# A matrix product with rotary embedding: weight chunks and the first four input tiles loaded in turn, and the early casts shared out anew

## The chip, the cores and the metric

The kernel runs on one core of one Trainium2 chip. The metric is the device time of one execution in microseconds (us). The span of a profile is some 2 us shorter than the device time of the same execution.

## The reference

```python
# x 16 x 512 x 768, weight 768 x 768, cos and sin 512 x 64, n_heads 12, all float32
y = np.matmul(x, weight).reshape(batch, seq, n_heads, head_dim)
y1, y2 = halves of the last axis of y
out1 = y1 * cos1 - y2 * sin1
out2 = y2 * cos2 + y1 * sin2
return np.concatenate([out1, out2], axis=-1).reshape(batch, seq, hidden)
```

## The kernel before

The input is cut into 64 tiles of 128 rows, taken as 32 pairs; (n, s) is tile s of pair n. A tile is loaded, cast to fp16, transposed by TensorE into PSUM in six blocks, copied back to SBUF, mostly by ScalarE, and multiplied with six weight chunks, each 128 x 768 (20 of the later tiles are transposed by VectorE instead). One tile with one chunk is a "tile-chunk": a 512-column and a 256-column product. VectorE then multiplies with cos and sin (the "rope"), GpSimd adds, and a store follows. The program order is fixed by hand. The change is in the start, where tiles one to four (pairs 0 and 1) meet weights that are still arriving. In this text tile five is (2, 0), tile six is (2, 1), and the weight chunks have the numbers 0 to 5.

```python
for n in (0, 1):
    load_pair(n)                     # tiles one to four
load_w(0, 0, 0, 256)                 # chunk 0 in two pieces
load_w(0, 0, 256, H)
for t, e in CHUNKS[1:]:
    load_w(t, e)                     # chunks 1 to 5
... cos, sin, then tiles five and on, all on one queue
warm(10)                             # products with zeros
cast(0, 0, nc.vector)
cast(0, 1, nc.scalar)
transpose(0, 0, nc.vector)           # the engine is that of the copy back
warm(2)
transpose(0, 1, nc.scalar)
cast(1, 0, nc.vector)
cast(1, 1, nc.scalar)
warm(2)
transpose(1, 0, nc.vector)
warm(3)
for c0, c1 in ((0, 256), (256, H)):
    cast_w(0, 0, c0, c1)
    mm(0, 0, 0, 0, c0, c1)
    mm(0, 1, 0, 0, c0, c1)
    if c0 == 0:
        transpose(1, 1, nc.scalar)
for k, c in enumerate(CHUNKS[1:]):
    cast_w(*c)
    if k < 2:
        mm(1, 0, *CHUNKS[k])
    mm(0, 0, *c)
    mm(0, 1, *c)
    if 1 < k < 4:
        mm(1, 0, *CHUNKS[k])
... VectorE prepares cos and sin
rope_pair(0)
upto("cast", 6)                      # ScalarE casts tiles five and six
for c in CHUNKS[4:]:
    mm(1, 0, *c)
for c in CHUNKS[:3]:
    mm(1, 1, *c)
upto("turn", 5)                      # tile five: transposes, ScalarE's copy back
for c in CHUNKS[3:]:
    mm(1, 1, *c)
rope_pair(1)
for n in range(2, NP):               # from here on as in the kernel after
    ...                              # tile five's product, tile six's transposes, ...
```

## Time and profile before

| what | before |
|---|---|
| time, median of three runs | 155.65 us (155.53 to 155.98) |
| span of the profile | 153.0 us |
| TensorE / VectorE / GpSimd / ScalarE busy | 96% / 85% / 81% / 50% |
| first VectorE cast of a whole weight chunk began | 9.66 us |
| last weight cast began | 13.64 us |
| tile five's cast on ScalarE began | 15.34 us |
| tile five's product on TensorE began | 17.97 us |

A line of the timeline has the start, the length, the engine (PE is TensorE's products, PEld its weight loads, DVE VectorE, ACT ScalarE), the source line, the operation with output and input, how many were merged, and in brackets the idle time before it with what ended it. A line of the chain of waits has the start, the length and who held the chain. The ends of products are modelled, starts are recorded; so where a small gap of TensorE matters below, it is taken from starts.

### The profile page before, as it was taken

What the parts mean: (1) busy time and instruction counts of PE and PEld (TensorE: products, weight loads), DVE (VectorE), ACT (ScalarE), POOL (GpSimd) and SP (SyncE); (2) the same over time, 40 slices, a digit from 0 to 9 for tenths busy, and PEclk for the clock granted to TensorE, in tenths of its full rate; (3) what the DMA queues carried; (4) which work ended last, traced back from release to release, by engine and by line L of the source; (5) the groups of instructions that cost most, each with busy time, mean ns of one, the idle gap of its engine ahead of it and who ended that gap; (6) DMA issues with size and microseconds to landing.
All of it is one profiled execution on the core that took longest, in us unless ns stands there. A gap on an engine that the chain in (4) does not pass through costs nothing.

```text
span 153.0 us, 2768 instructions
## 1 busy us (share of the span) xinstructions
PE 146.4 (96%) x1062; PEld 92.8 (61%) x1062; DVE 129.9 (85%) x136; ACT 76.8 (50%) x95; POOL 123.6 (81%) x72
## 2 busy tenths in 40 slices
PE   6999999999999999999999999999999999999970
PEld 2355678666666566666666566666656666666640
DVE  0656999777798998989898989989898987987991
ACT  3440696867444824283445726254616648876200
POOL 1000399999997999799997999787897879899990
PEclk9999999999999999999999999999999999999998
DMA  4999999999999999999999999999999937896555
GB/s 141 352 409 396 402 384 322 237 349 361 349 338 382 330 330 320 344 350 402 346 326 351 390 366 321 351 387 391 408 415 416 412 141 301 327 365 245 207 206 206
DMA packets 27437, 51.17 MB, mean 334 GB/s; under 512 B 7200, under 2 KB 12960, under 8 KB 27424
## 3 DMA queue, kind: packets, MB, share of 16 engines
q1 hardware_dynamic: 15040, 29.17, 54.7%
q10 hardware_dynamic: 6944, 19.86, 32.9%
q0 software_dynamic: 5440, 1.97, 10.5%
q8 instruction: 8, 0.13, 0.4%
q14 instruction: 5, 0.04, 0.1%
HBM read 27.79 MB, written 25.17 MB: 346 GB/s over the span
## 4 chain that ended last, share of the span: by engine, by line
PE 86%; DMA 5%; DVE 4%; SPq 2%; issue 1%; DVEq 0%
PE psy L174 77%; PE pt L140 9%; DMA w_raw<-in_weight_dram 5%; DVE tq L188 3%; SPq L123 1%; SPq L83 1%; DVE w_sb L126 0%; DVE psy L225 0%; DVE ov L229 0%; DVE tq L225 0%; DVEq L229 0%; DVEq L188 0%
## 5 line engine op out<-in xcount | busy, mean ns | idle before, releaser
L174 PE MATMUL psy<-w_sb,xT 128*128 128x256 f16 (+2 forms) x781 | 132.0, 323 | 0.4 <-DVE w_sb L126 0.4
L188 DVE TENSOR_TENSOR tq<-psy,csn 128x1024 f32<-128x1024 f32 (+1 forms) x99 | 111.9, 1169 | 12.1 <-PE psy L174 11.5
L199 POOL TENSOR_TENSOR ov<-tq 128x1536 f32<-128x1536 f32 (+2 forms) x45 | 111.4, 2505 | 8.7 <-DVE tq L188 4.1
L174 PEld LDWEIGHTS <-xT 128*128 128x128 f16 x781 | 74.6, 98 | 44.9 <-ACT xc L76 0.5
L76 ACT COPY xT<-pt 128x768 f16<-128x768 f16 x42 | 33.6, 800 | 53.4 <-PE pt L140 53.4
L76 ACT CAST xc<-xs 128x768 f16<-128x768 f32 x42 | 36.8, 904 | 12.3 <-DMA xs<-in_x_dram 11.0
L140 PEld LDWEIGHTS <-xc 128*128 128x128 f16 x264 | 18.1, 98 | 6.7 <-DVE xc L78 1.5
L140 PE MATMUL pt<-ident,xc 128*128 128x128 f16 x264 | 21.8, 219 | 0.3 <-DVE xc L78 0.2
L329 POOL COPY mark<-xs 128x1 f32<-128x1 f32 x1 | 0.2, 184 | 16.0 <-DMA xs<-in_x_dram 16.0
L99 POOL DMA_DIRECT2D xh<-in_x_dram x20 | 11.8, 595 | 0.5 <-issue 0.5
L76 ACT CAST xc<-xf 128x768 f16<-128x768 f32 x10 | 9.1, 906 | 0.0
L254 PE MATMUL psy<-cold 128*128 128x512 f16 x17 | 6.2, 515 | 1.2 <-DVE cold L261 1.2
L148 DVE STREAM_TRANSPOSE xT<-xh 128x384 f32<-128x384 f32 x10 | 7.0, 701 | 0.0
L148 DVE STREAM_TRANSPOSE xT<-xc 128x384 f32<-128x384 f32 x10 | 5.6, 562 | 0.0
L126 DVE CAST w_sb<-w_raw 128x768 f16<-128x768 f32 (+2 forms) x7 | 3.4, 500 | 2.2 <-DMA w_raw<-in_weight_dram 2.2
L78 DVE CAST xc<-xs 128x768 f16<-128x768 f32 x2 | 1.9, 948 | 3.4 <-DMA xs<-in_x_dram 3.4
L254 PEld LDWEIGHTS <-cold 128*128 128x128 f16 x17 | 1.9, 124 | 3.5 <-issue 2.2
L78 DVE COPY xT<-pt 128x768 f16<-128x768 f16 x2 | 1.1, 558 | 1.2 <-PE pt L140 1.2
L76 ACT ACT_TABLE_LOAD x1 | 1.3, 1283 | 0.7 <-PEq L405 0.7
L261 DVE MEMSET cold<- 128x256 uint32 x1 | 0.3, 272 | 0.9 <-PEq L405 0.9
L229 DVE TENSOR_TENSOR ov<-psy,tq 128x384 f32<-128x384 f32 x1 | 0.6, 558 | 0.0
L225 DVE TENSOR_TENSOR tq<-psy,csn 128x384 f32<-128x384 f32 x1 | 0.6, 556 | 0.0
(9 smaller groups left out, 1.9 us busy)
## 6 DMA issues: line engine op xcount, KB each, us to landing
out_dram<-ov ACTq DMA_DIRECT2D x25, 768.0 KB, 8.7
xs<-in_x_dram SPq DMA_DIRECT2D x44, 384.0 KB, 9.7
xf<-in_x_dram SPq DMA_DIRECT2D x20, 192.0 KB, 11.6
out_dram<-ov SPq DMA_DIRECT2D x7, 384.0 KB, 2.3
out_dram<-ov SPq DMA_DIRECT2D x3, 768.0 KB, 5.3
w_raw<-in_weight_dram SPq DMA_DIRECT2D x5, 384.0 KB, 7.0
xh<-in_x_dram POOLq DMA_DIRECT2D x20, 96.0 KB, 10.3
w_raw<-in_weight_dram SPq DMA_DIRECT2D x1, 256.0 KB, 5.6
```

The lines of the kernel that those rows point to most:

```text
L76: eng.copy(out=o, in_=i_)
L78: eng.tensor_copy(out=o, in_=i_)
L83: nc.sync.dma_start(out=xss[n, s], in_=x[b].rearrange("(p r) h -> r p h", r=SB)[r])
L99: eng.dma_start(out=dst[ts(q, R)], in_=src[r, q])
L123: nc.sync.dma_start(out=w_raw[t, e][:, c0:c1], in_=wv[t, e, :, c0:c1])
L126: nc.vector.tensor_copy(out=w_sb[:, t, e, c0:c1], in_=w_raw[t, e][:, c0:c1])
L140: nc.tensor.transpose(pt[:, t, e, :], xc[:, t, e, :], ident)
L148: nc.vector.transpose(out=xT.bitcast(FP32).rearrange("p t (j a) o -> p t j (a o)", j=NQ), in_=x16.pop((n, s)).bitcast(FP32).rearrange(orde ...
L174: nc.tensor.matmul(ps[:, a - lo : z - lo], xTT[n, s][:, t, e, :], w_sb[:, t, e, a:z], start=((t, e) == CHUNKS[0] and n > 1), stop=((t, e) ...
L188: nc.vector.tensor_tensor(out=tqs[n][:, :, c0:c1].rearrange("p j (h d) -> p j h d", d=D), in0=ps.rearrange("p (h d) -> p h d", d=D) .unsqu ...
L199: eng.tensor_tensor(out=ovs[n][:, ds(c0, w)].rearrange("p (h t d) -> p h t d", t=2, d=HD), in0=tq[:, 0].rearrange("p (h t d) -> p h t d", ...
L254: nc.tensor.matmul(psys[n][b], cold[:, 0:P], cold, start=True, stop=opened[0] < WARM - 6)
```

## The change

The intent: the weights arrive earlier relative to the tiles, so that TensorE has real products sooner and fewer products are left once the last chunk is in. Chunk 0 is no longer cut. Tile three is now cast by ScalarE, as tile four already was, so that VectorE is free when a chunk lands. Two products with zeros fill the wait for tile three.

```diff
-    for n in (0, 1):
-        load_pair(n)
-    load_w(0, 0, 0, 256)
-    load_w(0, 0, 256, H)
-    for t, e in CHUNKS[1:]:
-        load_w(t, e)
+    load_pair(0)
+    for k, c in enumerate(CHUNKS):
+        load_w(*c)
+        if k < 2:
+            load(1, k)
 ... (three products with zeros fewer)
-    cast(1, 0, nc.vector)
+    warm(WARM - 12)
+    cast_w(*CHUNKS[0])
+    mm(0, 0, *CHUNKS[0])
+    mm(0, 1, *CHUNKS[0])
+    cast(1, 0, nc.scalar)
+    cast_w(*CHUNKS[1])
+    idle(2)
+    transpose(1, 0, nc.vector)
+    mm(0, 0, *CHUNKS[1])
+    mm(0, 1, *CHUNKS[1])
     cast(1, 1, nc.scalar)
 ... (the old loops over the chunks go)
+    cast_w(*CHUNKS[2])
+    for c in CHUNKS[:2]:
+        mm(1, 0, *c)
+    transpose(1, 1, nc.scalar)
+    for k, c in enumerate(CHUNKS[2:]):
+        if k:
+            cast_w(*c)
         mm(0, 0, *c)
         mm(0, 1, *c)
-        if 1 < k < 4:
-            mm(1, 0, *CHUNKS[k])
+        if k == 0:
+            mm(1, 0, *c)
+        elif k < 3:
+            mm(1, 1, *CHUNKS[k - 1])
 ...
     upto("cast", 6)
-    for c in CHUNKS[4:]:
+    mm(1, 1, *CHUNKS[2])
+    for c in CHUNKS[3:]:
         mm(1, 0, *c)
-    for c in CHUNKS[:3]:
-        mm(1, 1, *c)
     upto("turn", 5)
     for c in CHUNKS[3:]:
         mm(1, 1, *c)
```

More of the change, by code (lines that the diff above doesn't have):

```diff
@@ L244, in store @@
         eng.dma_start(out=dst, in_=src)
-    WARM = 17
+    WARM = 14
     opened = [0]
@@ L257, in warm, with idle @@
             opened[0] += 1
+    def idle(k):
+        for _ in range(k):
+            nc.tensor.matmul(psys[1][2], cold[:, 0:P], cold, start=False, stop=False)
     ctx.enter_context(tc.manual_schedule())
@@ L303 @@
     transpose(0, 1, nc.scalar)
-    cast(1, 0, nc.vector)
-    cast(1, 1, nc.scalar)
-    warm(2)
-    transpose(1, 0, nc.vector)
-    warm(3)
-    for c0, c1 in ((0, 256), (256, H)):
-        cast_w(0, 0, c0, c1)
-        mm(0, 0, 0, 0, c0, c1)
-        mm(0, 1, 0, 0, c0, c1)
-        if c0 == 0:
-            transpose(1, 1, nc.scalar)
-    for k, c in enumerate(CHUNKS[1:]):
-        cast_w(*c)
-        if k < 2:
-            mm(1, 0, *CHUNKS[k])
+    warm(WARM - 12)
[8 more added lines that the diff above has]
+    mm(0, 1, *CHUNKS[1])
+    cast(1, 1, nc.scalar)
+    cast_w(*CHUNKS[2])
[5 more added lines that the diff above has]
+            cast_w(*c)
         mm(0, 0, *c)
         mm(0, 1, *c)
-        if 1 < k < 4:
-            mm(1, 0, *CHUNKS[k])
+        if k == 0:
+            mm(1, 0, *c)
+        elif k < 3:
+            mm(1, 1, *CHUNKS[k - 1])
     nc.vector.tensor_copy(out=csn[:, 1, :, 0:HD], in_=sin_sb[:, :, HD:D])
```

## The prediction

> **What bounds the kernel now.** I read the page first (busy shares and the slices), then the chain of waits in order of time, then the timeline of the first 20 us, and last the list of waits. The first line of the page gives the budget of each engine.
>
> ```profile
> PE 146.4 (96%) x1062; PEld 92.8 (61%) x1062; DVE 129.9 (85%) x136; ACT 76.8 (50%) x95; POOL 123.6 (81%) x72
> ```
>
> TensorE is busy 96% of a 153.0 us span; the next engine, VectorE, has 85%. The question for any change is whether TensorE's unbroken run can begin earlier, or do less after it has begun. The chain of waits says where that run begins (columns: start, length, what):
>
> ```profile
> 4.63 6.97 DMA w_raw<-in_weight_dram
> 11.63 0.57 DVE w_sb L126
> 12.24 4.45 PE psy L174 x26
> 16.69 0.34 PE pt L140 x6
> 17.02 1.77 PE psy L174 x12
> 18.80 0.34 PE pt L140 x6
> ```
>
> The chain is DMA until 11.60 us (the fourth weight chunk), one cast, and from 12.24 us TensorE alone, piece joining piece, to 143.38 us, where the final VectorE pieces take over. So the change, all of it in the first 18 us, is worth exactly the distance by which the run after those 18 us moves. What TensorE waits for around 16 to 19 us is in the timeline of that stretch (start, length, engine, line, work, idle time before it in brackets):
>
> ```profile
> 15.34 1.88 ACT L76 CAST xc<-xs 128x768 f16<-128x768 f32 x2 [4.90 <-DMA xs<-in_x_dram]
> 16.31 0.54 PEld L140 LDWEIGHTS <-xc 128*128 128x128 f16 x6
> 17.13 0.79 ACT L76 COPY xT<-pt 128x768 f16<-128x768 f16 x1
> 17.97 0.55 PEld L174 LDWEIGHTS <-xT 128*128 128x128 f16 x6 [0.35 <-ACT xT L76]
> ```
>
> This is what the reader should see: ScalarE sat idle 4.90 us for the fifth input tile, then cast tile five and tile six, one behind the other, then copied the transposed tile five out of PSUM, until 17.92 us. The weight load of the fifth tile's first product began at 17.97 us, having waited 0.35 us for that copy. TensorE was still finishing the fourth tile then (17.02 + half of an average tile product, 0.98, is 18.00 us), so the array itself lost nothing. But the margin is only some 0.03 us: the chain's TensorE pieces hide a second chain, load of tile five, two casts, one copy, which ends at the same moment.
>
> The casts of the weights show the rate at which loads land:
>
> ```profile
> 9.66 0.56 DVE L126 CAST w_sb<-w_raw 128x768 f16<-128x768 f32 x1 [0.48 <-DMA w_raw<-in_weight_dram]
> 10.64 0.56 DVE L126 CAST w_sb<-w_raw 128x768 f16<-128x768 f32 x1 [0.42 <-DMA w_raw<-in_weight_dram]
> 11.63 0.56 DVE L126 CAST w_sb<-w_raw 128x768 f16<-128x768 f32 x1 [0.43 <-DMA w_raw<-in_weight_dram]
> 12.61 0.56 DVE L126 CAST w_sb<-w_raw 128x768 f16<-128x768 f32 x1 [0.42 <-DMA w_raw<-in_weight_dram]
> 13.64 0.56 DVE L126 CAST w_sb<-w_raw 128x768 f16<-128x768 f32 x1 [0.47 <-DMA w_raw<-in_weight_dram]
> ```
>
> Each started on a landing. One 384 KB load lands every 0.98 to 1.03 us, with the DMA share at or near 1.0 in the window table from 4 us on: the start is bound by bytes, not by the issue, which runs 4 to 7 us ahead.
>
> **What the Trainium skill says.** "DMA: Bandwidth & Descriptors", section "Queues, rings and completion order", says that each DMA engine consumes the descriptors of a ring in order. The trace agrees for loads of one queue: tiles and weights land in the order of issue. Reordering therefore decides which load has which place in the line, not when the tenth is through. The same page, "Why small descriptors are slow", says that a packet carries a fixed cost. The trace agrees in size: its packet records show 121 ns for 3072 bytes, 84 ns for 2048 and 46 ns for 1024, so a row cut in two takes 130 ns. "TensorE: Matmul & The Clock Gate", section "Part 1: The HAM clock gate", says that the array runs at half rate until about 3.4 us of sustained activity, and falls back after an idle window of that length. The trace agrees: the first ten 512-column warm products take 0.424 us each (4.24 us for ten), the two after the first transposes about 0.22. "ScalarE: Activation LUTs", section "What ACT_TABLE_LOAD costs", gives 186 ns plus 0.833 ns per column; that makes 0.83 us for 768 columns as an estimate, and the trace has 0.80 for the copy and 0.90 for the cast.
>
> **The change part by part.**
>
> Loads. Before: four tiles, then the first weight chunk in two pieces (columns 0 to 255 and the rest), then five chunks. After: tile, tile, chunk 0, tile, chunk 1, tile, chunks 2 to 5. Both are ten 384 KB loads, so chunk 2 is seventh and chunk 5 tenth in both. Only chunks 0 and 1 come forward, and tiles three and four go back. Not cutting chunk 0 saves 130 - 121 = 9 ns on each of 8 rows per DMA engine, 0.07 us, and one completion write of 9 ns: all behind it lands 0.08 us earlier. Tile five is twelve full loads' worth of line behind; its issue waits for the eighth load before it (the order of instructions shows eight slots in turn), which in both kernels falls at about 8.6 us, well before the line is empty. I take its landing from 15.34 to 15.26 us.
>
> Weight cast. On VectorE, one 0.56 us cast for two that took 0.62; it moves from 8.56 us to about 6.6 (the third load lands at about 6.4, where the third tile landed before; VectorE ends its copy at 6.62). VectorE loses one 0.95 us tile cast to ScalarE, where it costs 0.89. ScalarE has room: its copy of tile two ends at 7.74, tile three lands by about 7.7, cast to 8.6; tile four lands at 9.6, cast to 10.5.
>
> Fill. Three of the 17 warm products (0.81 us for three) go and two neutral ones (0.43) come, in a place where TensorE would wait for the cast of tile three. No cost on the path.
>
> TensorE's order. One tile-chunk is a 512 and a 256 column product, 1.95 / 6 = 0.325 us. When the last chunk is cast (14.20 us), before had 14 of the 24 tile-chunks of the first four tiles behind it (five chunks of tiles one and two, four of tile three), ten to go. After has 15 (five each of tiles one and two, three of tile three, two of tile four), nine to go. Between the casts of chunks 3, 4 and 5 three tile-chunks fit, 0.975 us for a spacing of 1.0, in both. So TensorE reaches the transposes of tile five 0.325 us earlier, 16.69 - 0.33 = 16.36, plus up to 0.08 from the earlier landings, 16.28. The cast of tile five ends at about 16.17 to 16.25, so this still just fits. It then does three tile-chunks (0.34 + 0.98 us) and is ready for tile five's product at 17.6.
>
> There the gain stops. ScalarE still casts tiles five and six and then copies: 15.26 + 1.79 + 0.79 = 17.84 us, so the weights can be loaded at about 17.89 instead of 17.97, and the product begins about 17.94 instead of 18.02. Of 0.41 us that TensorE is ahead, 0.33 becomes a new wait for ScalarE. On the path: 0.08 us. Sum: 155.65 - 0.08 = 155.57; I say 155.5, leaning down a little because the casts of chunks 4 and 5 cost small gaps (26 products took 4.45 us where 13 x 0.325 is 4.23) that a different order may also close.
>
> After 18 us nothing differs: same instructions in the same order, and TensorE as the bound to 143.4.
>
> **The rivals.** (1) All 0.33 to 0.41 us come through, if tile six's cast does not stand before the copy, or the loads land faster in that run. It would give 155.2 to 155.3. Against it: the two casts ran back to back without a wait in between, and the order of ScalarE's instructions is unchanged there. (2) The tight new order backfires: tile four lands at 9.6 us, its cast ends at 10.5, its transposes stand in TensorE's queue ahead of chunk 2; a load delayed by a few tenths (one such dent is in the record, 221 GB/s at 5.5 us where 393 is usual) holds up chunk 2. It would cost up to 0.3 us, but the one tile-chunk of lead absorbs it: 155.6 to 155.8. (3) The clock falls: TensorE does less between 7.4 and 11.2 us, by my sum some 3.1 us of work in 3.8 (two neutral products, two transposed tiles, six tile-chunks), which I judge busy enough. If it fell for one window, 1 to 2 us would be lost, 156.5 to 157.5. I give that 1 to 2%. (4) A big gain of 1 us or more, since weights come two places earlier. Against it: the tenth load and tile five do not move, and TensorE works almost without a gap from 9.44 us already.
>
> **Range and chances.** Three runs before spread 155.53 to 155.98, so a median is good to about 0.2. Theory and rivals 1 and 2 span 155.2 to 155.8; with the spread I take 155.0 to 155.95. Two per cent is 3.1 us, ten times what can move: within 2% at 0.97, slower 0.015 for the clock, faster 0.015.
>
> **What would show it.** Right: the second and third weight loads land by 8.7 us, the fourth weight chunk's cast still starts at 11.5 to 11.6, tile five's ScalarE cast at 15.2 to 15.35; a new gap of about 0.3 us before the product of tile five, released by the ScalarE copy; from there the chain is TensorE alone, shifted by 0 to 0.15 us. Wrong: no such gap and a shift of 0.3 us or more (rival 1); gaps before chunks 2 to 5 that last beyond their casts (rival 2); warm products or tile-chunks after 8 us at double length (rival 3); or tile five landing more than 0.2 us away from 15.3, which would move everything.

## The result and the profile after

The changed kernel took 155.75 us (median of four runs, 155.62 to 155.88), the kernel before 155.72 (four runs, 155.53 to 155.98). The ratio is 1.0001, with a 95% interval from 0.9982 to 1.002: the same. A ratio here is the mean time of one kernel's fast runs over the mean of the other's of the same rounds, so it isn't quite the ratio of the medians quoted.

The busy line of the page hardly moves:

```profile
PE 147.1 (96%) x1060; PEld 93.2 (61%) x1060; DVE 129.1 (84%) x134; ACT 77.4 (50%) x96; POOL 123.6 (80%) x72
```

VectorE has two instructions fewer, one tile cast and one weight cast, and 0.8 us less; ScalarE has the tile cast. The chain of waits, from 3 to 20 us, shows the difference:

```profile
3.07 7.17 DMA xs<-in_x_dram
10.25 6.62 DMA xs<-in_x_dram
...
16.90 0.90 ACT xc L76
17.80 0.70 ACT xT L76
18.50 0.05 issue
18.55 0.83 PE psy L174 x6
```

Before, TensorE held the chain from 12.24 us on. Now it takes it over at 18.55 us, and until then the chain is the input loads and then ScalarE: tile six's cast, and the copy of tile five. From 18.55 us on it is TensorE alone again, piece joining piece as before, up to 143.96 us, where VectorE's last pieces take over. The second of the two DMA pieces ends at 16.87 us with the landing of tile six, not of tile five: the cast of tile six began 0.02 us after it. Where both tiles have landed, one cast of this trace begins 0.79 to 0.82 us after the one before; this one came 0.97 us after, so it waited some 0.17 us for its own tile. The kernel before shows the same (landing 16.30, cast 16.32 us).

The timeline of the same stretch shows what TensorE waits for:

```profile
15.93 1.87 ACT L76 CAST xc<-xs 128x768 f16<-128x768 f32 x2 [3.39 <-DMA xs<-in_x_dram]
16.87 0.34 PEld L140 LDWEIGHTS <-xc 128*128 128x128 f16 x6 [0.33 <-ACT xc L76]
17.22 1.14 PE L174 MATMUL psy<-w_sb,xT 128*128 128x256 f16 x6
17.70 0.79 ACT L76 COPY xT<-pt 128x768 f16<-128x768 f16 x1
18.54 0.55 PEld L174 LDWEIGHTS <-xT 128*128 128x128 f16 x6 [0.57 <-ACT xT L76]
18.55 0.83 PE L174 MATMUL psy<-w_sb,xT 128*128 128x256 f16 x6 [0.19 <-ACT xT L76]
```

There are two waits. At 16.87 us tile five's transposes wait for its cast. At 18.54 us its product waits for the copy. By starts, tile four's last product began at 17.98 us and gave the array free at 18.20 (a 512-column product follows another after 0.216 us here), so the array stood 0.35 us; at the transposes, by the same reckoning, 0.11 us. The kernel before, reckoned alike, had no wait at the transposes, but it had one at the product: tile four's last product began at 17.62 us, the array was free at 17.84, and tile five's product began at 17.97, after a copy that ended at 17.92. That is 0.13 us. So the new waits are 0.11 and 0.22 us, 0.33 together. The lead is as large: without its wait, tile five's transposes would have begun 2.56 us after the last weight cast began, against 2.89 before. The lead is there, and both waits give it back.

The casts of the last three chunks:

```profile
12.21 0.56 DVE L126 CAST w_sb<-w_raw 128x768 f16<-128x768 f32 x1 [0.42 <-DMA w_raw<-in_weight_dram]
13.20 0.56 DVE L126 CAST w_sb<-w_raw 128x768 f16<-128x768 f32 x1 [0.42 <-DMA w_raw<-in_weight_dram]
14.20 0.56 DVE L126 CAST w_sb<-w_raw 128x768 f16<-128x768 f32 x1 [0.44 <-DMA w_raw<-in_weight_dram]
```

They come every 0.99 to 1.00 us, as before, but in this trace 0.56 to 0.59 us later than in the trace of the kernel before, and tile five's cast 0.59 us later (15.93 against 15.34). Is that the change? If it were, the change would have cost 0.6 us somewhere, and the time doesn't show it. The experiments had to settle this first.

### The profile page after: what moved, and what is told of

Same layout as the page of the kernel before. It is cut to its first block, busy times and chain, and to the rows that moved or that the text cites. A ratio compares the mean times of both kernels' runs of the same rounds, so it can differ in the third digit from the quotient of the medians.

```text
span 153.6 us, 2763 instructions
## 1 busy us (share of the span) xinstructions
PE 147.1 (96%) x1060; PEld 93.2 (61%) x1060; DVE 129.1 (84%) x134; ACT 77.4 (50%) x96; POOL 123.6 (80%) x72
## 4 chain that ended last, share of the span: by engine, by line
PE 82%; DMA 9%; DVE 4%; SPq 1%; ACT 1%; issue 1%; DVEq 0%
PE psy L174 73%; DMA xs<-in_x_dram 9%; PE pt L140 9%; DVE tq L188 3%; SPq L83 1%; ACT xc L76 1%; SPq L123 1%; ACT xT L76 0%; DVE psy L225 0%; DVE ov L229 0%; DVE tq L225 0%; DVEq L229 0%; DVEq L188 0%
## 5 line engine op out<-in xcount | busy, mean ns | idle before, releaser
L76 ACT CAST xc<-xs 128x768 f16<-128x768 f32 x43 | 37.7, 904 | 10.3 <-DMA xs<-in_x_dram 10.2
L140 PEld LDWEIGHTS <-xc 128*128 128x128 f16 x264 | 18.6, 100 | 6.7 <-ACT xc L76 0.9
L140 PE MATMUL pt<-ident,xc 128*128 128x128 f16 x264 | 22.3, 222 | 0.0
L126 DVE CAST w_sb<-w_raw 128x768 f16<-128x768 f32 x6 | 3.4, 560 | 4.0 <-DMA w_raw<-in_weight_dram 4.0
L78 DVE CAST xc<-xs 128x768 f16<-128x768 f32 x1 | 1.0, 953 | 3.1 <-DMA xs<-in_x_dram 3.1
```

Source lines behind the costliest of these rows:

```text
L76: eng.copy(out=o, in_=i_)
L78: eng.tensor_copy(out=o, in_=i_)
L126: nc.vector.tensor_copy(out=w_sb[:, t, e, c0:c1], in_=w_raw[t, e][:, c0:c1])
L140: nc.tensor.transpose(pt[:, t, e, :], xc[:, t, e, :], ident)
```

## The experiments

To compare traces whose loads land at different times, I measure from A, the start of the last weight cast, which begins on the landing of chunk 5 in every trace (0.02 us after it; 0.09 with the weights in two pieces). All times in us, from the starts of the records; differences were taken before rounding. "Turn six" is the first of tile six's transposes.

| trace | A | tile five's cast - A | its product - A | turn six - A | span - A | span |
|---|---|---|---|---|---|---|
| before | 13.64 | 1.70 | 4.33 | 5.00 | 139.35 | 152.99 |
| before, again | 14.19 | 1.67 | 4.31 | 4.97 | 139.30 | 153.50 |
| before, copy first | 13.28 | 1.71 | 4.27 | 5.07 | 139.41 | 152.69 |
| after | 14.20 | 1.72 | 4.34 | 5.01 | 139.41 | 153.62 |
| after, again | 13.98 | 1.71 | 4.35 | 5.02 | 139.41 | 153.39 |
| after, no fill | 14.12 | 1.70 | 4.34 | 5.01 | 139.40 | 153.52 |
| after, copy first | 14.21 | 1.67 | 4.03 | 4.81 | 139.21 | 153.42 |
| after, tiles five and six early | 13.91 | 0.99 | 4.45 | 5.10 | 139.54 | 153.45 |
| after, tile five early, copy first | 14.05 | 0.99 | 3.95 | 4.73 | 139.15 | 153.20 |
| after, two more loads ahead of tile five | 14.30 | 2.47 | 5.10 | 5.77 | 140.03 | 154.33 |
| after, all weights in two pieces | 13.68 | 1.96 | 4.61 | 5.27 | 139.82 | 153.50 |
| after, tile five early, turn early | 13.40 | 1.04 | 3.94 | 4.60 | 139.00 | 152.40 |
| the same, again | 13.93 | 1.01 | 3.91 | 4.57 | 138.97 | 152.90 |

After turn six the rows hardly differ: VectorE's last instruction ends 131.26 to 131.30 us after it in all thirteen traces. The last store lands 2.02 to 2.07 us later, again in all. Only the closing instructions after that landing differ from kernel to kernel: 1.03 us in the three traces of the old order of loads, 1.09 in the changed kernel and most of its variants, 0.97 with two more loads, 1.21 with all weights in two pieces. So 0.06 to 0.12 us of a difference in span - A can belong to the ending of the program and not to the start; why the ending differs isn't shown.

The theory under test: the lead that TensorE gains before tile five is taken back by a second chain, the landing of tile five, ScalarE's casts of tiles five and six, and its copy of tile five. (By the chain above the landing of tile six belongs to it too; the theory rests on tile six's cast standing ahead of the copy.) Rivals: the end is set by something after 18 us; the new order of loads is itself slower; the clock; a wait for VectorE's rope or for ScalarE's next tile that stands just behind.

### The changed kernel once more (repeat_after)

No edit.

> The changed kernel once more, unaltered, for a second trace and five rounds against the kernel before. My theory (the end is set by the landing of tile five and three ScalarE operations behind it): ratio to before between 0.998 and 1.002, and in this trace again a wait of the weight load for the ScalarE copy of tile five, 0.3 to 0.6 us; the start of tile five's product lags the landing of tile five by 2.6 us (0.90 + 0.90 + 0.79 us of ScalarE) as in the first trace. If the late landing of tile five in the first trace (15.93 us against 15.34) belongs to the new order of loads, it is again above 15.8; if it is chance of the run, it is elsewhere between 15.2 and 16.

Measured: 155.41 us (155.23 to 156.57), before on the same chip 155.52 (154.95 to 156.18); ratio 1.0005, interval 0.9975 to 1.0036. The trace has the same waits: 0.59 us of the weight load and 0.20 of TensorE for the copy. The product begins 2.64 us after tile five's cast did (2.62 in the first trace). Tile five's cast began at 15.69 us, between the two values seen so far, which did not meet the "above 15.8" that I had set for a slower order.

### The kernel before once more (repeat_before)

No edit.

> The kernel before, unaltered, for a second trace. If the line of loads alone varies from run to run, the last weight cast begins somewhere between 13.2 and 14.2 us here too, and the span ends 139.4 us after it, within 0.05. If it is again at 13.6 or below, with the changed kernel's three traces so far at 13.9 to 14.2, the new order of loads delays the line by some 0.3 us.

Measured: the last weight cast began at 14.19 us, so the kernel before too has runs as late as the changed one's 14.20; one run took 155.64 us. Its span ended 139.30 us after that, against 139.35 in the first trace and 139.4, within 0.05, expected. The line of loads, then, is what varies: by 0.9 us over the first three and the fourth to sixth row of the table (13.28 to 14.20), while span - A stays between 139.30 and 139.41. The rival of a slower order isn't needed for the 0.6 us between the first two traces, though six traces do not exclude a smaller effect of the order.

### ScalarE's copy of tile five ahead of its cast of tile six (copy_first)

```diff
-    upto("cast", 6)
+    upto("cast", 5)
     ...
     upto("turn", 5)
+    upto("cast", 6)
```

> The changed kernel with ScalarE's cast of tile six moved behind its copy of tile five. My theory: the 0.9 us cast leaves the chain, tile five's product then waits for nothing but TensorE's own order and starts within 1.8 us of the landing of tile five, 0.2 to 0.6 us earlier than in the changed kernel; time 0.2 to 0.4 us under before (ratio 0.997 to 0.9985). Rival (the loads alone, or work after 18 us, set the end): no change, ratio 0.999 to 1.001. Second rival (the gain is handed to the next wait, ScalarE being late for tile six or seven): a new wait of the same size at 19 to 23 us and no gain.

The timeline of this kernel from 15.5 to 20 us:

```profile
17.39 0.80 ACT L76 COPY xT<-pt 128x768 f16<-128x768 f16 x1 [0.60 <-PE pt L140]
18.08 0.89 ACT L76 CAST xc<-xs 128x768 f16<-128x768 f32 x1
18.24 0.55 PEld L174 LDWEIGHTS <-xT 128*128 128x128 f16 x6 [0.30 <-ACT xT L76]
19.02 0.34 PEld L140 LDWEIGHTS <-xc 128*128 128x128 f16 x6 [0.24 <-ACT xc L76]
```

The product of tile five begins 2.35 us after its cast in place of 2.62, and 0.32 us earlier from A (4.03 against 4.34). So the cast of tile six stood on the path, as said; but I had expected the product within 1.8 us of the landing, and that was wrong: three tile-chunks of tile four lie between the transposes and the product. Nor is the wait for the copy gone: by starts the array still stands 0.08 us before the product, since transposes and copy take a little longer than those three tile-chunks. Then the last line shows the second rival: tile six's cast, now later, holds the weight load of its transposes for 0.24 us (0.12 us by the starts of the transposes). Of 0.32 us, 0.19 are left at turn six, and 0.21 at the end of the span (139.21 against 139.41). Both the theory and the handing on to the next wait are true, each for a part. Time: 155.15 us (154.63 to 155.64), ratio 0.9974, interval 0.9946 to 1.0002: not clear of 1.

### The same edit in the kernel before (copy_first_before)

> The same edit in the kernel before. My theory: there TensorE is itself busy until the copy is done (margin 0.03 us), so moving the cast gives nothing: ratio 0.999 to 1.001, tile five's product still at about 18.0 us. If the edit gives 0.2 us or more here too, ScalarE was on the path of the kernel before by more than I read from its trace, and the new load order is not what makes the room.

From A the product moves by 0.03 to 0.06 us (4.27 against 4.33 and 4.31), turn six comes later (5.07 against 5.00 and 4.97), and the span ends 0.06 to 0.11 us later. The wait for the copy there shrinks by starts from 0.13 and 0.11 to 0.08 us, which is all that the edit gives. So there is hardly any room for it without the new order: that is the theory's point. The time would have told another story: 155.18 us (154.84 to 155.71), ratio 0.998, interval 0.9955 to 1.0004, nearly as low as the run above. Its traced run simply had the earliest line of loads of all, A at 13.28 us. A difference of 0.3 us between medians of six runs is not evidence here.

### Tiles five and six ahead of cos and sin (tile5_early)

```diff
+    load_pair(2)
     nc.sync.dma_start(out=csn[:, 0], in_=cos...)
     nc.sync.dma_start(out=sin_sb, in_=sin...)
-    for n in range(2, AHEAD):
+    for n in range(3, AHEAD):
```

> The changed kernel with tiles five and six loaded ahead of cos and sin (256 KB, 0.65 us of the line). My theory: tile five lands 0.6 us earlier, ScalarE is done before TensorE, the wait for the copy vanishes and the product of tile five starts 0.3 to 0.6 us earlier; time 0.2 to 0.4 us under before (ratio 0.997 to 0.9985). VectorE's first rope starts 0.7 to 0.9 us later, which I expect to be hidden. Rival (VectorE's later start holds PSUM banks or GpSimd back): gaps of TensorE at 18 to 30 us, time the same as before or above.

Tile five's cast began 0.73 us earlier from A (0.99 against 1.72), and yet the product began later (4.45 against 4.34). The timeline from 16 to 19 us tells why:

```profile
16.63 0.23 DVE L335 COPY csn<-sin_sb 128x128 f32<-128x128 f32 x1 [2.15 <-DMA sin_sb<-in_sin_dram]
17.09 2.36 DVE L188 TENSOR_TENSOR tq<-psy,csn 128x1024 f32<-128x1024 f32 x2
17.86 0.10 PEld L174 LDWEIGHTS <-xT 128*128 128x128 f16 x1 [0.30 <-ACT xT L76]
18.36 0.81 PE L174 MATMUL psy<-w_sb,xT 128*128 128x256 f16 x6 [0.42 <-DVE tq L188]
```

Weights of the product were loaded at 17.86 us, but the product waited until 18.36 for VectorE's first rope. There are six PSUM banks for results, three to a pair, so tile five's first bank is the one that the first rope empties. That rope began at 17.09 us because sin was now behind two whole tiles: 2 us later, not the 0.7 to 0.9 that I wrote (I had counted the 0.65 us that the tiles gain, not the two loads that sin loses). The rival was right, and my expectation wrong in its size and in its sign. Time 155.72 us (155.49 to 156.14), ratio 1.0018, interval 0.9994 to 1.0042.

### Tile five alone ahead of cos and sin, and the copy first (five_early_copy_first)

```diff
+    load(2, 0)
     nc.sync.dma_start(out=csn[:, 0], in_=cos...)
     nc.sync.dma_start(out=sin_sb, in_=sin...)
-    for n in range(2, AHEAD):
+    load(2, 1)
+    for n in range(3, AHEAD):
     ...                               # and the edit of copy_first
```

> The changed kernel with tile five alone loaded ahead of cos and sin (tile six stays behind them, so that the rope starts one load later and not two) and ScalarE's cast of tile six behind its copy of tile five. My theory now: the trace from the cast of the last weight chunk to the end of tile six's transposes, 5.50 us in the kernel before and 5.51 in both traces of the changed kernel, becomes 5.0 to 5.2 us, TensorE neither waiting for ScalarE's copy nor for VectorE's rope; time 0.3 to 0.5 us under before (ratio 0.9968 to 0.998). Rival (the rope, now about 1 us later, still holds the PSUM bank, as it did with two tiles ahead): a wait for VectorE before tile five's product and 5.4 us or more. Second rival (TensorE's later run gives the gain back): 5.1 us there, but the span still ends 139.4 us after the last weight cast began.

The product begins 3.95 us after A, 0.39 earlier than in the changed kernel, without a wait for the rope; for the copy the array still stands 0.08 us by starts, as in copy_first. From A to the end of tile six's transposes it is 5.24 us, a little over the 5.0 to 5.2 expected: turn six still waited for its cast. The span ended after 139.15 us, so what is gained at 19 us is kept to the end, and the second rival falls. Time 155.17 us (154.87 to 155.74), ratio 0.998, interval 0.9953 to 1.0007.

### Two loads that nobody uses ahead of tile five (late_tile5)

```diff
+    for k in (0, 1):
+        nc.sync.dma_start(out=extra[:, k], in_=cos...)
     for n in range(2, AHEAD):
         load_pair(n)
```

> The changed kernel with two loads of 128 KB that nobody uses between sin and tile five (cos again, into a spare buffer). By the packet records 8 packets of 46 ns on each engine, twice: about 0.75 us of the line. My theory: the casts of the weights do not move against the start of the line, tile five lands about 0.75 us later, TensorE waits for tile five at its transposes and at its product, and the span ends about 140.1 us after the last weight cast began in place of 139.4. Rival (the last weight chunk alone sets the end, tile five has slack): 139.4 to 139.5.

The timeline from 14 to 20.5 us (lines of the source are one further down in this kernel):

```profile
16.77 1.89 ACT L77 CAST xc<-xs 128x768 f16<-128x768 f32 x2 [4.12 <-DMA xs<-in_x_dram]
17.71 0.51 PE L141 MATMUL pt<-ident,xc 128*128 128x128 f16 x6 [0.68 <-ACT xc L77]
19.41 0.83 PE L175 MATMUL psy<-w_sb,xT 128*128 128x256 f16 x6 [0.21 <-ACT xT L77]
```

Tile five's cast comes 0.75 us later from A (2.47 against 1.72), its product 0.76, turn six 0.76, VectorE's last instruction 0.76, and the end of the span 0.62 (140.03; 140.1 was expected). Chunk 5 alone does not set the end: tile five has no slack, and what it is late for is paid in full up to VectorE's last instruction. Of the 0.14 us regained behind it, 0.12 lie in the program's closing instructions.

### Without the two neutral products (no_fill)

```diff
-    idle(2)
```

> The changed kernel without the two neutral products ahead of tile three's transposes. My theory: they stand in a wait, so the span still ends 139.4 us after the last weight cast began. Rival (they hold the clock up): tile-chunks after 8 us take 0.65 us in place of 0.325, and the span grows by 1 us or more.

Span - A is 139.40, the product at 4.34, and turn six at 5.01, as ever: no sign of a lower clock after 8 us. The fill costs nothing and, in this one trace, holds nothing up.

### Every weight chunk in two pieces (split_weights)

```diff
-        load_w(*c)
+        load_w(*c, 0, 256)
+        load_w(*c, 256, H)
```

> The changed kernel with every weight chunk loaded in two pieces, columns 0 to 255 and the rest, as the kernel before did for the first chunk alone. By my step of 130 ns for the two packets of a row against 121 for one, each chunk costs the line 0.07 to 0.08 us more. From the landing of chunk 2 to that of chunk 5 are three chunks: 3.00 us in the kernel before, 2.96 in the changed one by the starts of their casts; I expect 3.18 to 3.25 here, and the span still to end 139.4 us after the last weight cast began. Rival (the packets' fixed cost is hidden, or the splitting costs issue time and slots): 2.95 to 3.05, or well above 3.3.

The cast of chunk 2 began at 10.52 us and that of chunk 5 at 13.68: 3.16 us for three chunks, against 2.96 in the changed kernel (11.24 to 14.20). That just misses the 3.18 to 3.25 expected; against the 2.93 to 3.00 of the other traces it is 0.05 to 0.08 us a chunk, about the 0.07 to 0.08 of the step. The rest of the expectation failed: the span ended 139.82 us after A, not 139.4. Of the 0.41 us more, 0.24 come between A and tile five's cast (1.96 against 1.72), and 0.12 in the closing instructions. The DMA engines were busy all the while (1.01 to 1.08 of their time in the window table from 12.5 to 16 us), so the line was not short of loads; why tile five lands later against chunk 5 stays open.

### The transposes of tile five two tile-chunks earlier as well (turn_early, turn_early_again)

```diff
     mm(1, 1, *CHUNKS[2])
-    for c in CHUNKS[3:]:
-        mm(1, 0, *c)
+    mm(1, 0, *CHUNKS[3])
     upto("turn", 5)
     upto("cast", 6)
+    for c in CHUNKS[4:]:
+        mm(1, 0, *c)
     for c in CHUNKS[3:]:
         mm(1, 1, *c)
     ...                               # on top of five_early_copy_first
```

> The version with tile five ahead of cos and sin and the copy of tile five ahead of tile six's cast, and now also tile five's transposes two tile-chunks earlier in TensorE's order. There tile six's transposes still waited for their cast: they began 0.79 us after tile five's product in place of 0.66. My theory: that wait goes too, tile six's transposes begin 4.60 to 4.65 us after the last weight cast began (4.74 in that version, 5.00 to 5.02 in the changed kernel), and the span ends 139.0 us after the last weight cast began, 0.4 us less than the changed kernel. Time 0.2 to 0.5 us under before, ratio 0.997 to 0.999; the interval of six runs will be near 0.25% wide on each side, since the line of loads varies by up to 0.9 us, so the trace decides. Rival: tile five's cast is too late for the earlier place, TensorE waits for it, and the span ends 139.2 us or more after that cast.

> The same version once more, for a second set of times on whatever chip comes up: the first set gave a ratio of 0.999 with an interval from 0.9961 to 1.002, which does not separate 0.4 us from nothing. My theory: the span again ends 139.0 us after the last weight cast began, whatever the line of loads does, and the mean time is 0.2 to 0.5 us under before. If the mean is at or above before again, the 0.4 us of the trace is not seen in the time and I do not call the version faster.

The timeline of the first of the two, from 13.5 to 20.5 us:

```profile
15.92 0.80 ACT L76 COPY xT<-pt 128x768 f16<-128x768 f16 x1 [0.60 <-PE pt L140]
16.62 0.90 ACT L76 CAST xc<-xs 128x768 f16<-128x768 f32 x1
17.89 0.43 PEld L140 LDWEIGHTS <-xc 128*128 128x128 f16 x6
18.00 0.50 PE L140 MATMUL pt<-ident,xc 128*128 128x128 f16 x6
```

ScalarE has tile five's copy and tile six's cast done at 17.52 us, and tile six's transposes begin without a wait, 4.60 us after A (4.57 in the second trace). The spans end 139.00 and 138.97 us after A: 0.41 to 0.44 less than the changed kernel, in both. That is nearly all of the 0.46 us for which the array stood at tile five in the changed kernel: the lead that the change had made and could not keep, and most of the 0.13 us that the kernel before lost too. These edits together were not tried in the kernel before; by the starts of its products not much over those 0.13 us could be gained there.

The time is less clear. The two sets gave 155.06 us (154.41 to 156.02) and 154.96 (154.64 to 156.56), before 155.43 and 155.46; the ratios are 0.999 (0.9961 to 1.002) and 0.9989 (0.9948 to 1.0031). The medians are 0.37 and 0.50 us lower, but each set has one run at 156 us or above, which lifts its mean. The mean is under before by 0.16 us or so, less than the 0.2 to 0.5 expected. By the traces this version does 0.4 us less after the last weights land; by the times it can't be called faster.

## Why the prediction was right, point by point

**No gain from the early order, because ScalarE's chain takes it back: right and shown.** TensorE does reach tile five earlier. The working put its lead at 0.33 us from its own order, 0.41 with the loads, and the new wait at 0.33. By starts the lead is 0.33 us and the new waits are 0.33: 0.11 before the transposes, and 0.22 more than before at the product. Relative to A the product stands where it was: 4.34 and 4.35 after, 4.33 and 4.31 before. Moving the cast of tile six (copy_first) and moving the landing of tile five (late_tile5, five_early_copy_first) move the product as the theory says, and the first edit gives next to nothing in the kernel before (0.03 to 0.06 us at the product, nothing at the end).

**The margin of 0.03 us in the kernel before: misread.** The working let tile four's products start at 17.02 us and end at 18.00, just behind the copy. The first of them began at 16.86, and by starts the array stood 0.13 us for the copy. So ScalarE ended last there already, and a lead of TensorE alone could give nothing: the mechanism holds the better for it.

**The two casts "back to back": misread, and the sum right by luck.** From the start of tile five's cast to the end of its copy the working has 2.58 us; both first traces have 2.57. But it left out the 0.17 us for which the second cast waited for tile six, and that each of ScalarE's operations begins 0.09 to 0.12 us before the end of a cast ahead of it when nothing holds it. The two slips cancel.

**"This still just fits", at tile five's transposes: not quite.** The transposes waited for the cast, 0.11 us of the array. The step compared two sums of a tenth of a microsecond's accuracy; the cast won by a little. It changed nothing, since the copy was the later wait.

**0.08 us earlier from the uncut chunk 0: right as a cost per chunk, not visible in the time.** Cutting chunks costs 0.05 to 0.08 us each (split_weights). The prediction's "agrees in size" says too much, though: in the Trainium skill, "DMA: Bandwidth & Descriptors", the section cited, "Why small descriptors are slow (HBM only)", gives the fixed cost of a packet as about three cycles, with 32 bytes a cycle. The packet records have 37 ns for 1024 bytes more, so three cycles are 3.5 ns by estimate, where the records leave 9. And the line of loads varies by 0.9 us from run to run, while the tail after A was 0.05 to 0.11 us longer in the changed kernel's traces (139.40 to 139.41 against 139.30 and 139.35). Of that, 0.06 us lie in the closing instructions (1.09 us against 1.03); up to VectorE's last instruction the two kernels differ by 0.01 to 0.04 us from A.

**The landings in absolute time: wrong.** The working let chunk 3's cast start at 11.5 to 11.6 us and tile five's at 15.2 to 15.35; the traces of the changed kernel have 12.01 to 12.21 and 15.69 to 15.93. The second and third weight loads were to land by 8.7 us; in the first trace they landed at 9.27 and 11.21. For the third the sign contradicts the working itself, which leaves chunk 2 in seventh place (10.62 us in the kernel before). The step took the landings of one trace for fixed. The repeat of the kernel before, with its last weight cast at 14.19 us, shows that they aren't.

**The clock: no loss, but a late rise.** Tile-chunks after 8 us are at full rate with and without the fill. The granted clock rose from half to full at 5.10 us in the first trace before, 3.9 us after the first product, which is near the 3.4 us of sustained work that the prediction cites; in the two traces of the changed kernel it rose only at 7.21 and 7.12 us, some 6 us after. In all thirteen traces it rose at 4.15 to 5.50 us nine times and at 6.94 to 7.21 us four times. The other two late ones are tile5_early and split_weights; the early ones include no_fill at 4.65, whose times from A are those of the changed kernel. So the late rise cost nothing here; why it comes isn't shown.

**Same time:** 155.5 was forecast with 155.0 to 155.95; 155.75 was measured. So wide a range around "no change" would have been met by other mechanisms as well; it is the traces that speak for this one.

## What to carry to other kernels

When an engine looks like the only bound, look for a second chain that ends at the same moment: here TensorE by starts already stood 0.13 us for ScalarE's copy in the kernel before, so a lead for TensorE alone was worth nothing. Order the helper engine by who waits for it: the copy that the next product needs goes ahead of the cast for the product after that. And where the start depends on DMA, measure from a landing in the trace, not from the start of the run: that made 0.2 us visible here under a run-to-run variation of 0.9.

## What the Trainium skill lacked or had wrong

- "DMA: Bandwidth & Descriptors", section "Latency and other measured facts", gives 0.2 us on average and up to 2 us at high load for an access to HBM. Packets of 3072 bytes that usually took 121 ns took up to 0.93 us in the first trace of the kernel before, and up to 1.6 us in that of the changed kernel. The size fits the page, though no run shows that this is the cause. What the page lacks is that it comes in the first microseconds of a run: from 10 to 20 us none of these two traces took over 0.15 us. The landing of chunk 5 varies by 0.9 us between runs of nearly the same loads. In the three traces of the old order of loads, what packets took beyond the usual in the first 9 us comes to 0.77, 1.03 and 1.21 us an engine, in the order of A (13.28, 13.64, 14.19): a part of that variation, it seems, but no run isolates it.
- "ScalarE: Activation LUTs", section "What ACT_TABLE_LOAD costs", gives one time for fp32 and bf16, an estimate of 0.83 us for 768 columns. The copy of fp16 out of PSUM took 0.80 us, the cast of fp32 out of SBUF 0.88 to 0.91; on a chain of three such operations the difference is worth counting. The cast also reads its columns with a stride; whether type, memory or stride makes the difference no run shows.
- No page that I read works out how work of ScalarE for a later tile holds back a lead of TensorE: tile six's cast of 0.9 us ahead of tile five's copy took the whole lead of 0.33 us.
